# An RWKV layer rearranged: key products, paired tiles, triangular solves on another engine, merges on another DMA queue

## The chip, the cores and the metric

The kernel runs on one core of one Trainium2 chip. The metric is device time in microseconds of one launch. A core has TensorE (matrix products into PSUM), VectorE, ScalarE and GpSimd (elementwise work on SBUF; GpSimd doesn't read PSUM), SyncE, which here only issues DMAs, and 16 DMA engines. In the profile they are PE (its weight loads PEld), DVE, ACT, POOL and SP. Each engine works through its own list of instructions in order and waits on semaphores for the others.

## What is computed

The whole kernel is a decoder of two layers on 1024 positions of width 1024 in fp32: layer 0 with a gated linear recurrence, layer 1 with RWKV-7 time mixing, each followed by cross-attention into a memory and a squared-ReLU MLP. Only the time mixing matters here:

```
xx = x_prev - x
r = (x + xx * mu[0]) @ w_rkv[0];  k = (x + xx * mu[2]) @ w_rkv[1];  v = (x + xx * mu[3]) @ w_rkv[2]
w_log = -softplus(-(w0 + tanh(xw @ w1) @ w2)) - 0.5;  decay = exp(-exp(w_log));  a = sigmoid(a0 + (xa @ a1) @ a2)
kk = k * k_k, normalised per head;  k = k * (1 + (a - 1) * k_a)
rem_a, rem_b = -kk, kk * a
# per head and step:
sa = state @ a_t
state = state * w_t + sa b_t^T + v_t k_t^T
y_t = state @ r_t
```

The recurrence runs in chunks of 64 positions. For a chunk the mutual effect of the `a` and `b` vectors needs the inverse of a triangular 64x64 matrix per head. It is built from two 32x32 inverses, found by substitution (the "solves"), and an off-diagonal block, found by two small products (the "merges").

## The kernel before, in words

Everything lies transposed: 128 channels (two heads) by 1024 positions, so the 1024 channels are eight tiles f = 0..7. fp32 matrices are split into a rounded part and a rest, and each product is three matmuls (`mm3`, L304 to L306). `split` (L203 cast on ScalarE, L204 subtraction on VectorE) is used for weights and activations.

The layer's order is: low-rank maps; then for each tile f `decay(f)` (12 matmuls, the decay's running product `P`, its inverse `IP`, and `a`), `fphase` of k (48 matmuls: eight k-steps by three, for each half of the positions) and `prep(f, pk)`, which takes k from PSUM. `prep` makes `kk`, its square `sq` for the norm, `at` (minus kk times the decay before the position; L1181 and, for the first position of each chunk, L1182), `a` (a times kk times IP; L1179 and L1184 on GpSimd) and `kp` (L1175, L1176, and L1185 on GpSimd), and stores them for the scan. `sums(f)` puts eight matmuls against `ind` between those of the next tile (through the list `between`); `gram(f)` forms the 64x64 products (L1217), scales them by the norms (L1218, which waits for a small DMA into `db`) and stores the 32x32 blocks to `Ld` and `Mod`.

Then eight r tiles (the last two as a pair) and eight v tiles (the first two as a pair), each 48 matmuls; `evac_r` (L1325) multiplies by P and stores; `evac_v` transposes v (L1366), forms the bonus (L1358, then L1377, which needs r and k loaded back by `early`) and the gate. Then the scan, from L1555 on, over 16 chunks.

Before each of k, r and v the inputs are mixed: `rwkv_make_mix` makes the eight 512-wide pieces of one half of the positions in four groups (L1054 on ScalarE, L1055 and, in the second half, the one-column L1057 on VectorE, then `split`). A half's mix is called either through `later` (run between the two halves of a tile) or after a tile.

Aside from that run the solves, four of them (q = tiles 2q and 2q+1): `solve_load` (L1230, two memsets), `solve` (31 steps of two instructions, L1243 and L1245, and the copy L1246), `solve_store` (L1250, L1251); and the merges: `merge_load` (L1262 to L1264, per tile eight DMAs with 32x16 pieces of 128 bytes), `merge` (L1277, ScalarE copies, L1284), `merge_store` (L1292). `aside(step)` calls them at steps listed by hand: steps 0 to 7 follow the key tiles, 8 to 13 the first six r tiles, 14 the last pair, 15 and on the v tiles. Solve 0 runs on GpSimd, the others on VectorE. All their DMAs are issued by SP, whose queue also carries the weight tiles (L235), the loads of `early` and every store.

A scheduler orders each engine's list by a simulated timeline; `behind()` adds edges that put what it covers behind everything traced so far on the same engine. All 128x1024 tiles come from one pool of 45 buffers; weights are split two tiles ahead and loaded three ahead (`DA`).

Of the kernel before, what the change touches and what calls it, by code (L numbers as in the profile page):

```python
# [991 lines left out]


SL, SO, ST = (6, 7, 9, 11), (7, 8, 10, 12), (12, 10, 12, 14)
ML, ME, MS = (13, 11, 13, 15), (14, 12, 14, 16), (15, 13, 15, 17)
SE = [lambda nc: nc.gpsimd] + [lambda nc: nc.vector] * 3
# [6 lines left out]
def rwkv_consts(self):  # L1003
    nc = self.nc
    c = self.const
    self.omu = c([128, 48], "omu")
    nc.vector.tensor_scalar(self.omu, self.colv("mu", 48), -1.0, 1.0, ALU.mult, ALU.add)
    self.w0h = c([128, 8], "w0h")
    nc.vector.tensor_scalar(self.w0h, self.colv("w0"), 0.5, None, ALU.mult)
    self.a0h = c([128, 8], "a0h")  # L1010
    nc.vector.tensor_scalar(self.a0h, self.colv("a0"), 0.5, None, ALU.mult)
    self.kah = c([128, 8], "kah")
    nc.vector.tensor_scalar(self.kah, self.colv("k_a"), 0.5, None, ALU.mult)
    self.kam = c([128, 8], "kam")
    nc.vector.tensor_scalar(self.kam, self.colv("k_a"), -1.0, 1.0, ALU.mult, ALU.add)

    self.ind = c([128, 2], "ind")
    nc.gpsimd.memset(self.ind, 0.0)
    nc.gpsimd.memset(self.ind[0:64, 0:1], 1.0)
    nc.gpsimd.memset(self.ind[64:128, 1:2], 1.0)  # L1020

    self.id64 = c([128, 64], "id64")
    nc.vector.tensor_add(self.id64, self.ident[:, 0:64], self.ident[:, 64:128])

    self.mask1 = c([128, 128], "mask1")
    nc.gpsimd.memset(self.mask1, 1.0)
    self.mask2 = c([128, 64], "mask2")
    nc.gpsimd.memset(self.mask2, 1.0)
    for h in range(2):
        r = slice(h * 64, h * 64 + 64)  # L1030

        nc.gpsimd.affine_select(self.mask1[r, 0:64], self.mask1[r, 0:64], pattern=[[1, 64]], base=0,
                                channel_multiplier=-1, compare_op=ALU.is_ge, fill=0.0)
        nc.gpsimd.affine_select(self.mask2[r, :], self.mask2[r, :], pattern=[[1, 64]], base=-1,
                                channel_multiplier=-1, compare_op=ALU.is_ge, fill=0.0)
    self.db = c([128, 256], "db")
    self.pc = c([128, 128], "pc")

    self.ones = c([128, 128], "ones")
    nc.gpsimd.memset(self.ones, 0.0)  # L1040
    for h in range(2):
        nc.gpsimd.memset(self.ones[h * 64:h * 64 + 64, h * 64:h * 64 + 64], 1.0)


def rwkv_make_mix(self, X, i, hf):

    nc = self.nc
    out = []
    for j in range(KT // 2):
        m = self.unit()  # L1050
        for k in (2 * j, 2 * j + 1):
            o = (k % 2) * 512
            mu = self.col("mu", i * 8 + k)
            nc.scalar.activation(m[:, o:o + 512], X[hf][:, k, :], AF.Copy, scale=self.omu[:, i * 8 + k:i * 8 + k + 1])  # L1054
            nc.vector.scalar_tensor_tensor(m[:, o + 1:o + 512], X[hf][:, k, :511], mu, m[:, o + 1:o + 512], ALU.mult, ALU.add)  # L1055
            if hf:
                nc.vector.scalar_tensor_tensor(m[:, o:o + 1], X[0][:, k, 511:512], mu, m[:, o:o + 1], ALU.mult, ALU.add)  # L1057
        h, l = self.split(m)
        out += [(h[:, s], l[:, s]) for s in (slice(0, 512), slice(512, 1024))]
    return out  # L1060
# [31 lines left out]
def rwkv(self, X, xt, lw_wa, lw_g, post):  # L1092
# [20 lines left out]
    xk = []  # L1113
    for hf in range(2):
# [18 lines left out]
        xk.append(rwkv_make_mix(self, X, 2, hf))  # L1133
# [34 lines left out]
    def prep(f, pk):  # L1168
        cs = slice(f * 128, f * 128 + 128)
        c1 = lambda t: t[:, f:f + 1]  # L1170
        a, P, IP = dk.pop(f)
        kk = self.unit()
        nc.scalar.activation(kk, pk, AF.Copy, scale=self.col("k_k", f))
        kp = self.unit()
        nc.vector.tensor_scalar(kp, a, self.col("k_a", f), c1(self.kam), ALU.mult, ALU.add)  # L1175
        nc.vector.tensor_mul(kp, kp, pk)  # L1176
        sq = self.unit()
        nc.scalar.activation(sq, kk, AF.Square)
        nc.gpsimd.tensor_tensor(a, a, kk, ALU.mult)  # L1179
        at = kk  # L1180
        nc.vector.scalar_tensor_tensor(ch(at)[:, :, 1:], ch(kk)[:, :, 1:], -1.0, ch(P)[:, :, :63], ALU.mult, ALU.mult)  # L1181
        nc.vector.tensor_scalar(at[:, ::64], kk[:, ::64], -1.0, None, ALU.mult)  # L1182
        nc.sync.dma_start(MVd[:, f, 0, :], at)
        nc.gpsimd.tensor_tensor(a, a, IP, ALU.mult)  # L1184
        nc.gpsimd.tensor_tensor(kp, kp, IP, ALU.mult)  # L1185
# [3 lines left out]
        st_k[f] = sq, a, at  # L1189

# [36 lines left out]
    def solve_load(q):  # L1227
        sol[q] = [self.unit() for _ in range(3)]
        L, xt_, tmp = sol[q]
        nc.sync.dma_start(L, Ld[q].rearrange("b q h c s t -> (b q h c) (s t)"))  # L1230
        SE[q](nc).memset(xt_, 0.0)
        SE[q](nc).memset(xt_[:, ::33], 1.0)

    def solve(q):
# [5 lines left out]
        for s in range(31):  # L1240
            n, m = s + 1, 31 - s
            tv = tmp[:, :n * m].rearrange("p (j t) -> p j t", t=m)
            eng.tensor_tensor(tv, xv_[:, 0:n, s:s + 1].broadcast_to([128, n, m]),  # L1243
                              Lv[:, s:s + 1, s + 1:].broadcast_to([128, n, m]), ALU.mult)
            eng.tensor_tensor(xv_[:, 0:n, s + 1:], xv_[:, 0:n, s + 1:], tv, ALU.add)  # L1245
        eng.tensor_copy(tmp[0:64].rearrange("p (s j) -> p s j", j=32), xt_[0:64].rearrange("p (j s) -> p s j", s=32))  # L1246

    def solve_store(q):
        L, xt_, tmp = sol.pop(q)
        nc.sync.dma_start(Xd[q].rearrange("b q h c s t -> (b q h c) (s t)"), xt_)  # L1250
        nc.sync.dma_start(Xnd[2 * q:2 * q + 2].rearrange("q h c s t -> (q h c) (s t)"), tmp[0:64])  # L1251

    def merge_load(q):
        for f in (2 * q, 2 * q + 1):
            XT = self.unit()
            nc.vector.memset(XT, 0.0)
            XN = self.unit()
            xc = ch(XT)
            for h in range(2):
                for b in range(2):  # L1260
                    rs = slice(h * 64 + b * 32, h * 64 + b * 32 + 32)
                    nc.sync.dma_start(xc[rs, :, b * 32:b * 32 + 32], Xd[q, b, f % 2, h].rearrange("c s t -> s c t"))  # L1262
                nc.sync.dma_start(XN[h * 64:h * 64 + 32, 0:512].rearrange("p (c t) -> p c t", t=32), Xnd[f, h].rearrange("c s t -> s c t"))
                nc.sync.dma_start(XN[h * 64:h * 64 + 32, 512:1024].rearrange("p (c t) -> p c t", t=32), Mod[f, h])  # L1264
            mg[f] = XN, XT

    def merge(q):
        for f in (2 * q, 2 * q + 1):
            XN, XT = mg.pop(f)
            xc = ch(XT)  # L1270
            r0 = [slice(h * 64, h * 64 + 32) for h in range(2)]
            r1 = [slice(h * 64 + 32, h * 64 + 64) for h in range(2)]
            ps = self.bank()
            for c in range(16):
                s = slice(c * 32, c * 32 + 32)
                for h in range(2):
                    mm(ps[r1[h], s], XN[r0[h], 512 + c * 32:544 + c * 32], XN[r0[h], s], start=True, stop=True, tile_position=(h * 64, h * 64 + 32))  # L1277
            for h in range(2):
                nc.scalar.copy(XN[r1[h], 512:1024], ps[r1[h], :])
            ps = self.bank()  # L1280
            for c in range(16):
                s = slice(c * 32, c * 32 + 32)
                for h in range(2):
                    mm(ps[r0[h], s], XN[r1[h], 512 + c * 32:544 + c * 32], xc[r1[h], c, 32:64],  # L1284
                       start=True, stop=True, tile_position=(h * 64 + 32, h * 64))
            for h in range(2):
                nc.scalar.copy(xc[r0[h], :, 32:64], ps[r0[h], :].rearrange("p (c t) -> p c t", t=32))
            xts[f] = XT

    def merge_store(q):  # L1290
        for f in (2 * q, 2 * q + 1):
            nc.sync.dma_start(XTd[:, f, :], xts.pop(f))  # L1292

    def aside(step):

        for fn, steps in ((merge_store, MS), (merge, ME), (merge_load, ML), (solve_store, ST), (solve, SO), (solve_load, SL)):
            for q in range(4):
                if steps[q] == step:
                    with self.behind():
                        fn(q)  # L1300

    self.depth, self.ahead = DA
    xr, xv = [], []
    for f in range(8):
        decay(f)
        if f == 7:

            self.later.append(lambda: xr.append(rwkv_make_mix(self, X, 0, 0)))
        if f:
            sums(f - 1)  # L1310
        self.fphase(I["b_w_rkv"][0, 1], [f], xk, prep)
        if f:
            gram(f - 1)
        aside(f)


    xr.append(rwkv_make_mix(self, X, 0, 1))
# [10 lines left out]
    turns = [[f] for f in range(6)] + [[6, 7]]  # L1328
    for fs in turns:
        for f in fs:  # L1330
            early(f)
        if len(fs) > 1:
            self.later.append(lambda: xv.append(rwkv_make_mix(self, X, 3, 0)))
        if fs[0] == 0:
            sums(7)
        self.fphase(I["b_w_rkv"][0, 0], fs, xr, evac_r)
        if fs[0] == 0:
            gram(7)
        aside(8 + fs[0])


    xv.append(rwkv_make_mix(self, X, 3, 1))
# [181 lines left out]
    for fs in turns:  # L1524
# [3 lines left out]
        aside(14 + fs[-1])  # L1528
# [127 lines left out]
```

## Time and profile before

| | |
|---|---|
| median of 3 runs | 3068.84 us (3067.94 to 3074.63) |
| the profiled execution | 3074.59 us, its span 3072.8 us |
| mean granted TensorE clock | 0.970 |
| busy share | PE 94%, DVE 61%, ACT 44%, POOL 36% |
| RWKV key, r and v tiles up to the scan | 1424.6 to 1880.3 us of the span |
| key tile evacuated (L1173), tiles 0, 1, 2 | 1424.6, 1438.8, 1460.9 us |
| scan, its first W product to the last | from 1880.3 us, to about 2062 us |

In the rows, a line of the order of time has the start in us, the duration in us, engine, line, operation, out<-in (buffer numbers left out), shapes and count; in brackets, where there is one, the engine's idle time before it and what ended it. The granted clock is a share of TensorE's full speed: 1.00 is the level of 2.4 GHz, 0.50 that of 1.2 GHz.

### The profile page before, as it was taken

The numbers are of one execution on the slowest core, as the hardware profiler recorded it, in microseconds if no ns is written. First come the engines' busy times: TensorE is split into PE (matmuls) and PEld (weight loads), VectorE is DVE, ScalarE is ACT, GpSimd is POOL, SyncE is SP. The second block draws the span as 40 slices with busy tenths as digits, with TensorE's granted clock in tenths as the row PEclk, the third lists the DMA queues.
The fourth block names the chain that finished last, engine by engine and source line by source line (L and its number), as shares of the span: only waits on it lengthen the run. The fifth ranks groups of instructions, "written<-read, shape, count | busy, mean of one in ns | idle before, by whom it ended". The sixth has DMA issues, their size and how long they took to land.

```text
span 3072.8 us, 42865 instructions
## 1 busy us (share of the span) xinstructions
PE 2889.2 (94%) x16987; PEld 2394.9 (78%) x16987; DVE 1864.2 (61%) x2146; ACT 1344.2 (44%) x1915; POOL 1098.1 (36%) x909
## 2 busy tenths in 40 slices
PE   7999999898999999989987788989999899999998
PEld 6887898786888878867866666878788778887886
DVE  5576542637444778767788625884345644568776
ACT  5465342635454643355431523443334545454332
POOL 2000100015666744442461003662001466667442
PEclk9999999998999999999998899999999999999999
DMA  8213270123446644342664679872312245455443
GB/s 260 68 42 103 83 230 28 55 83 91 161 154 205 220 158 151 96 137 77 157 172 139 175 209 242 181 163 87 107 31 86 83 134 160 152 200 198 158 143 117
DMA packets 394921, 421.93 MB, mean 137 GB/s; under 512 B 103536, under 2 KB 305504, under 8 KB 394720
## 3 DMA queue, kind: packets, MB, share of 16 engines
q1 hardware_dynamic: 384720, 384.96, 42.4%
q0 software_dynamic: 9536, 33.64, 2.8%
q8 instruction: 134, 2.20, 0.3%
q14 instruction: 67, 0.55, 0.1%
q10 hardware_dynamic: 464, 0.59, 0.1%
HBM read 284.31 MB, written 134.74 MB: 136 GB/s over the span
## 4 chain that ended last, share of the span: by engine, by line
PE 54%; DVE 8%; issue 5%; POOL 4%; ACT 2%; DMA 2%; SPq 1%; POOLq 0%; DVEq 0%; ACTq 0%
PE q L304 12%; PE q L305 12%; PE q L306 12%; PE p L304 4%; PE p L305 4%; PE p L306 4%; DVE u L204 3%; PE q L1466 1%; ACT u L203 1%; DVE u L1245 1%; DVE u L1243 1%; DMA u<-d 1%; POOL u L1564 1%; PE q L1377 1%; DVE u L1577 1%
## 5 line engine op out<-in xcount | busy, mean ns | idle before, releaser
L204 DVE TENSOR_TENSOR u<-u,u 128x1024 fp32r<-128x1024 f32 (+1 forms) x518 | 812.2, 1596 | 351.4 <-ACT u L203 335.0
L304 PE MATMUL p<-u,u 128*128 128x512 f32 (+1 forms) x1920 | 722.2, 379 | 31.0 <-ACT u L203 26.3
L203 ACT CAST u<-u 128x1024 fp32r<-128x1024 f32 (+1 forms) x550 | 542.0, 1024 | 470.0 <-PE q L305 159.7
L305 PE MATMUL p<-u,u 128*128 128x512 f32 (+1 forms) x1920 | 721.0, 376 | 9.6 <-DVE u L204 9.6
L306 PE MATMUL p<-u,u 128*128 128x512 f32 (+1 forms) x1920 | 717.1, 374 | 3.8 <-DVE u L204 3.7
L304 PE MATMUL q<-u,u 128*128 128x512 f32 (+1 forms) x1632 | 643.9, 395 | 30.3 <-ACT u L203 9.2
L305 PE MATMUL q<-u,u 128*128 128x512 f32 (+1 forms) x1632 | 641.0, 393 | 6.4 <-DVE u L204 6.4
L306 PE MATMUL q<-u,u 128*128 128x512 f32 (+1 forms) x1632 | 635.8, 392 | 0.0
L304 PEld LDWEIGHTS p<-u,u 128*128 128x128 f32 x1920 | 368.7, 193 | 100.2 <-ACT u L203 31.8
L305 PEld LDWEIGHTS p<-u,u 128*128 128x128 f32 x1920 | 369.2, 192 | 76.1 <-DVE u L204 15.1
L306 PEld LDWEIGHTS p<-u,u 128*128 128x128 f32 x1920 | 369.1, 192 | 68.0 <-DVE u L204 5.8
L315 POOL TENSOR_SCALAR s<-s 128x1 f32<-128x1 f32 x98 | 37.2, 379 | 997.2 <-ACT u L313 996.2
L304 PEld LDWEIGHTS q<-u,u 128*128 128x128 f32 (+1 forms) x1632 | 309.4, 190 | 101.8 <-ACT u L203 13.9
L305 PEld LDWEIGHTS q<-u,u 128*128 128x128 f32 (+1 forms) x1632 | 309.9, 190 | 73.2 <-DVE u L204 8.7
L306 PEld LDWEIGHTS q<-u,u 128*128 128x128 f32 (+1 forms) x1632 | 309.7, 190 | 65.4 <-issue 0.4
L431 POOL TENSOR_TENSOR u<-u,u 128x1024 f32<-128x1024 f32 x64 | 179.2, 2822 | 84.8 <-DVE u L204 78.7
L975 DVE TENSOR_TENSOR z<-z,q 128x512 f32<-128x512 f32 x192 | 129.0, 681 | 94.2 <-PE q L306 93.8
L204 POOL TENSOR_TENSOR u<-u,u 128x1024 fp32r<-128x1024 f32 x32 | 95.1, 2971 | 166.3 <-ACT u L203 104.2
L411 POOL TENSOR_TENSOR u<-u,u 128x512 f32<-128x512 f32 x96 | 150.8, 1579 | 2.9
L304 PE MATMUL q<-z,u 128*128 128x512 f32 x256 | 102.6, 401 | 7.0 <-DVE u L610 7.0
L610 DVE SCALAR_TENSOR_TENSOR u<-p,s,u 128x1024 f32<-128x1024 f32 x24 | 30.8, 1284 | 122.3 <-ACT u L203 78.2
L204 DVE TENSOR_TENSOR u<-p,u 128x1024 fp32r<-128x1024 f32 x32 | 38.9, 1221 | 108.6 <-ACT u L203 108.6
(256 smaller groups left out, 3550.9 us busy)
## 6 DMA issues: line engine op xcount, KB each, us to landing
u<-d SPq DMA_DIRECT2D x201, 512.0 KB, 4.7
d<-u SPq DMA_DIRECT2D x113, 512.0 KB, 3.6
d<-u SPq DMA_DIRECT2D x132, 256.0 KB, 3.6
u<-in_m_w_up SPq DMA_DIRECT2D x64, 512.0 KB, 5.6
d<-u POOLq DMA_DIRECT2D x64, 512.0 KB, 4.3
u<-in_m_w_down SPq DMA_DIRECT2D x64, 512.0 KB, 6.0
u<-in_c_w_kv SPq DMA_DIRECT2D x32, 512.0 KB, 6.4
u<-d SPq DMA_DIRECT2D x56, 256.0 KB, 6.3
```

What stands on the lines that cost most here:

```text
L203: self.nc.scalar.copy(hv, src)
L204: (eng or self.nc.vector).tensor_tensor(lv, src, hv, ALU.subtract)
L304: mm(o, ah, bh, start=first, stop=False, **kw)
L305: mm(o, ah, bl, start=False, stop=False, **kw)
L306: mm(o, al, bh, start=False, stop=last, **kw)
L315: nc.gpsimd.tensor_scalar(v, ss, 1.0 / n, eps, ALU.mult, ALU.add)
L411: sub = lambda o, x, y: nc.gpsimd.tensor_tensor(o, x, y, ALU.subtract)
L431: self.nc.gpsimd.tensor_tensor(f[o][i], f[x][i], f[y][i], ALU.subtract)
L610: nc.vector.scalar_tensor_tensor(o, src, r, gb, ALU.mult, ALU.mult)
L975: nc.vector.tensor_add(to_, to_, o)
L1243: eng.tensor_tensor(tv, xv_[:, 0:n, s:s + 1].broadcast_to([128, n, m]), Lv[:, s:s + 1, s + 1:].broadcast_to([128, n, m]), ALU.mult)
L1245: eng.tensor_tensor(xv_[:, 0:n, s + 1:], xv_[:, 0:n, s + 1:], tv, ALU.add)
```

## The change

- Key products. `prep` is cut in two. `prep_head` makes `at` with a negated k_k column (`nkk`) and forms `IP * k` from PSUM at once; `prep_rest` makes `kp` (a scaled a times `IP * k`), `a` (one fused instruction), and multiplies `at` by the decay with one instruction, since minus is in already and the first position of a chunk needs nothing. GpSimd has no instruction left in it.
- Tiles. The last two key tiles and the first two r tiles run as pairs. `decay` runs one turn ahead. Half of the first r mix is built between the halves of the key pair, the rest, gram(5) and the second half's mix after `prep_head(7)` and ahead of `prep_rest(6)` and `(7)`; sums and grams of 6 and 7 move to the r tiles 2 and 3. Three of four groups of the first v mix are built in the last r pair, the fourth after it. The one-column piece of a mix moves from VectorE to ScalarE.
- Solves. Solves 0, 1 and 2 run on GpSimd, called behind key tiles 2, 4 and the key pair (their instructions are not put `behind`); their loads too are issued by GpSimd. Solve 3 stays on VectorE, its 31 steps spread one by one between the matmuls of r tiles 4 to 7; its memsets are on GpSimd.
- Merges. They go tile by tile, one per step: loads at steps 9 to 16, products one step later, stores one more. Steps 0 to 6 are now the key turns, 7 to 12 the r turns ([0, 1], 2, 3, 4, 5, [6, 7]), 13 to 19 the v turns. Memset, loads, stores of solves and merges are issued by GpSimd.

The diff, cut:

```diff
+TURNS = [[f] for f in range(6)] + [[6, 7]]
-SL, SO, ST = (6, 7, 9, 11), (7, 8, 10, 12), (12, 10, 12, 14)
-ML, ME, MS = (13, 11, 13, 15), (14, 12, 14, 16), (15, 13, 15, 17)
-SE = [lambda nc: nc.gpsimd] + [lambda nc: nc.vector] * 3
+SL, SO, ST = (2, 4, 6, 9), (2, 4, 6, 9), (2, 4, 6, 12)
+ML, ME, MS = range(9, 17), range(10, 18), range(11, 19)
+SE = [lambda nc: nc.gpsimd] * 3 + [lambda nc: nc.vector]
...
+            if hf:
+                nc.scalar.activation(m[:, o:o + 1], X[0][:, k, 511:512], AF.Identity, scale=mu, bias=m[:, o:o + 1])
             nc.vector.scalar_tensor_tensor(m[:, o + 1:o + 512], X[hf][:, k, :511], mu, m[:, o + 1:o + 512], ALU.mult, ALU.add)
-            if hf:
-                nc.vector.scalar_tensor_tensor(m[:, o:o + 1], X[0][:, k, 511:512], mu, m[:, o:o + 1], ALU.mult, ALU.add)
...
+    def prep_head(f, pk):
+        a, P, IP = dk[f]
+        at = self.unit()
+        nc.scalar.activation(at, pk, AF.Copy, scale=self.nkk[:, f:f + 1])
+        nc.vector.tensor_mul(IP, IP, pk)
+        dk[f] = a, P, IP, at
+
+    def prep_rest(f):
+        a, P, IP, at = dk.pop(f)
         kp = self.unit()
-        nc.vector.tensor_scalar(kp, a, self.col("k_a", f), c1(self.kam), ALU.mult, ALU.add)
-        nc.vector.tensor_mul(kp, kp, pk)
+        nc.vector.tensor_scalar(kp, a, self.col("k_a", f), self.kam[:, f:f + 1], ALU.mult, ALU.add)
         sq = self.unit()
-        nc.scalar.activation(sq, kk, AF.Square)
-        nc.gpsimd.tensor_tensor(a, a, kk, ALU.mult)
-        at = kk
-        nc.vector.scalar_tensor_tensor(ch(at)[:, :, 1:], ch(kk)[:, :, 1:], -1.0, ch(P)[:, :, :63], ALU.mult, ALU.mult)
-        nc.vector.tensor_scalar(at[:, ::64], kk[:, ::64], -1.0, None, ALU.mult)
+        nc.scalar.activation(sq, at, AF.Square)
+        nc.vector.scalar_tensor_tensor(a, a, self.col("k_k", f), IP, ALU.mult, ALU.mult)
+        nc.vector.tensor_mul(ch(at)[:, :, 1:], ch(at)[:, :, 1:], ch(P)[:, :, :63])
         nc.sync.dma_start(MVd[:, f, 0, :], at)
-        nc.gpsimd.tensor_tensor(a, a, IP, ALU.mult)
-        nc.gpsimd.tensor_tensor(kp, kp, IP, ALU.mult)
+        nc.vector.tensor_mul(kp, kp, IP)
...
+    def prep(f, pk):
+        prep_head(f, pk)
+        if f < 6:
+            prep_rest(f)
+        if f == 7:
+            rwkv_make_mix(self, X, 0, 0, xr[0], range(2, 4))
+            gram(5)
+            rwkv_make_mix(self, X, 0, 1, xr[1])
+            prep_rest(6)
+            prep_rest(7)
...
-        nc.sync.dma_start(L, Ld[q].rearrange("b q h c s t -> (b q h c) (s t)"))
-        SE[q](nc).memset(xt_, 0.0)
+        (nc.sync if q == 3 else nc.gpsimd).dma_start(L, Ld[q].rearrange("b q h c s t -> (b q h c) (s t)"))
+        nc.gpsimd.memset(xt_, 0.0)
...
+        for s in range(31):
+            if q == 3:
+                self.between.append(lambda s=s: one(s))
+            else:
+                one(s)
...
-                    nc.sync.dma_start(xc[rs, :, b * 32:b * 32 + 32], Xd[q, b, f % 2, h].rearrange("c s t -> s c t"))
+                nc.gpsimd.dma_start(xc[rs, :, b * 32:b * 32 + 32], Xd[f // 2, b, f % 2, h].rearrange("c s t -> s c t"))
...
-        for fn, steps in ((merge_store, MS), (merge, ME), (merge_load, ML), (solve_store, ST), (solve, SO), (solve_load, SL)):
+        for fn, steps in ((solve_load, SL), (solve, SO), (solve_store, ST), (merge, ME), (merge_load, ML), (merge_store, MS)):
...
-    for f in range(8):
-        decay(f)
+    decay(0)
+    for i, fs in enumerate(TURNS):
+        for f in TURNS[i + 1] if i < 6 else []:
+            decay(f)
+        if len(fs) > 1:
+            self.later.append(lambda: rwkv_make_mix(self, X, 0, 0, xr[0], range(2)))
+        if i:
+            sums(fs[0] - 1)
+        self.fphase(I["b_w_rkv"][0, 1], fs, xk, prep)
+        if 0 < i < 6:
+            gram(fs[0] - 1)
+        aside(i)
...
-    turns = [[f] for f in range(6)] + [[6, 7]]
+    for i, fs in enumerate([[0, 1], [2], [3], [4], [5], [6, 7]]):
...
+        if i in (1, 2):
+            sums(5 + i)
         self.fphase(I["b_w_rkv"][0, 0], fs, xr, evac_r)
+        if i in (1, 2):
+            gram(5 + i)
+        aside(len(TURNS) + i)
```

## Rows read from the trace of the kernel before

**Rows 1.** The page, part 1: busy time, share of the span, instructions.

```profile
PE 2889.2 (94%) x16987; PEld 2394.9 (78%) x16987; DVE 1864.2 (61%) x2146; ACT 1344.2 (44%) x1915; POOL 1098.1 (36%) x909
```

**Rows 2.** Stretches: length; busy PE, PEld, DVE, ACT, POOL; granted clock, DMA share, GB/s.

```profile
1424.60:1534.00 109.40, 104.26 (x753) 84.17 (x753) 81.49 (x68) 47.73 (x61) 48.76 (x18) 0.95 0.56 150
1534.00:1600.50 66.50, 57.65 (x389) 43.77 (x389) 51.27 (x64) 30.87 (x39) 41.23 (x37) 0.90 0.56 149
1600.50:1700.60 100.10, 75.22 (x601) 61.58 (x600) 84.72 (x201) 8.82 (x12) 24.58 (x34) 0.86 0.59 164
1700.60:1856.30 155.70, 135.55 (x1214) 103.76 (x1214) 67.13 (x89) 66.38 (x95) 5.12 (x4) 0.94 0.72 198
1856.30:1880.30 24.00, 11.86 (x59) 8.67 (x60) 9.34 (x18) 6.98 (x18) 9.65 (x11) 0.78 0.90 264
```

**Rows 3.** Waits of PE, 1424.6 to 1880.3: us in total, times, longest.

```profile
PE q L1377 <- DVE u L1358: 13.0, 2, 7.1
```

**Rows 4.** PE in order of time: ten matmul starts (first, last) and three waits.

```profile
1483.80 0.39 PE L305 MATMUL p<-u,u 128*128 128x512 f32 x1
...
1485.84 0.39 PE L305 MATMUL p<-u,u 128*128 128x512 f32 x1
...
1448.66 0.79 PE L304 MATMUL q<-u,u 64*128 64x512 f32 x1 [5.14 <-DVE u L1218]
...
1653.33 0.31 PE L1277 MATMUL q<-u 32*32 32x32 f32 x2 [10.59 <-DMA u<-d]
...
1707.34 1.22 PE L304 MATMUL p<-u,u 128*128 128x512 f32 x2 [13.74 <-ACT u L203]
```

**Rows 5.** SP's DMA issues in order of time: 32 merge loads (first, last), then weights.

```profile
1677.01 1.25 SPq L1262 DMA_DIRECT2D u<-d  x2
...
1694.54 0.48 SPq L1264 DMA_DIRECT2D u<-d  x1
...
1696.01 1.06 SPq L235 DMA_DIRECT2D u<-in_b_w_rkv  x2
```

**Rows 6.** DVE, then POOL, in order of time, in `prep(1)`.

```profile
1442.42 3.35 DVE L1181 SCALAR_TENSOR_TENSOR u<-u,u 128x1008 f32<-128x1008 f32 x1 [1.26 <-DMA d<-u]
1445.70 2.31 DVE L1182 TENSOR_SCALAR u<-u 128x16 f32<-128x16 f32 x1
...
1442.35 2.37 POOL L1185 TENSOR_TENSOR u<-u,u 128x1024 f32<-128x1024 f32 x1
1444.67 3.30 POOL L1184 TENSOR_TENSOR u<-u,u 128x1024 f32<-128x1024 f32 x1
```

**Rows 7.** DVE in order of time: two groups of a mix, split to split.

```profile
1556.75 1.23 DVE L204 TENSOR_TENSOR u<-u,u 128x1024 fp32r<-128x1024 f32 x1 [1.11 <-ACT u L203]
...
1560.41 1.23 DVE L204 TENSOR_TENSOR u<-u,u 128x1024 fp32r<-128x1024 f32 x1 [1.11 <-ACT u L203]
```

**Rows 8.** POOL in order of time, solve 0: first step, two between, last, copy.

```profile
1570.86 0.24 POOL L1243 TENSOR_TENSOR u<-u,u 128x31 f32<-128x31 f32 x1
...
1578.43 0.43 POOL L1245 TENSOR_TENSOR u<-u,u 128x112 f32<-128x112 f32 x1
...
1587.66 0.58 POOL L1245 TENSOR_TENSOR u<-u,u 128x207 f32<-128x207 f32 x1
...
1625.20 0.34 POOL L1245 TENSOR_TENSOR u<-u,u 128x31 f32<-128x31 f32 x1
1625.60 2.09 POOL L1246 COPY u<-u 64x1024 f32<-64x1024 f32 x1
```

**Rows 9.** ACT in order of time: key tile 2 taken from PSUM.

```profile
1460.89 1.11 ACT L1173 ACTIVATE u<-p,colt 128x1024 f32<-128x1024 f32 x1 [5.49 <-PE p L306]
```

**Rows 10.** DMA issues, columns: count, KB each, median us from issue to landing.

```profile
u<-d SPq DMA_DIRECT2D x201, 512.0 KB, 4.7
...
u<-d SPq DMA_DIRECT2D x64, 64.0 KB, 2.4
```

**Rows 11.** One line's instructions, GpSimd's DMA issue: ns min/median/max, first and last start.

```profile
L928 POOL DMA_DIRECT2D d<-u x32: 727/727/823, 769.0 to 2785.8; - x32
```

## What the change should do, and how that was worked out

> **What bounds the kernel now.** I read the busy shares first: TensorE is busy 94% of the span, VectorE 61%, GpSimd 36% [rows 1]. TensorE is the bound on average, so the change can win only where TensorE stands still or runs slowly. It touches the RWKV layer alone. I cut the part of that layer that it touches, from the end of the first key tile (1424.6 us) to the start of the recurrent scan (1880.3), into five stretches [rows 2]: key tiles 1 to 6; key tile 7 with r tiles 0 and 1; r tiles 2 to 7; the v tiles; what runs up to the scan.
>
> In each, length minus PE busy is idle time, and busy time times (1 - granted clock) is what the clock costs. The five rows give 10.4, 14.6, 35.4, 28.3 and 14.7 us, **103 us together** (71 idle, 32 clock). That is all that can be recovered here; outside, the instructions are nearly the same.
>
> What holds TensorE there, the waits and the order of time say. At 1448.66 it waits 5.1 us for L1218; at 1653.33 it waits 10.6 us for the loads of a merge; at 1707.34 it waits 13.7 us for a cast of weights [rows 4]. A further 13.0 us go to two releases of L1377, which are v tiles whose r and k were loaded late [rows 3]. Behind most of these stands the SP queue: merge loads take it from 1677.01 to 1695.02, 32 issues at 0.56 us, and only at 1696.01 is the next weight tile asked for [rows 5].
>
> **Part 1: key products.** Per tile three 128x1024 products leave GpSimd, an awkward pair (L1181, L1182) leaves VectorE, and two plain full-width products come to VectorE. What the old form costs stands in [rows 6]: L1181 starts at 1442.42, while GpSimd's L1185 runs to 1444.72, and ends 1.05 us after that. GpSimd's L1184, begun at 1444.67, needs 3.30 us instead of 2.37. L1182, 16 elements a partition, takes 2.31 us and ends when L1184 does. The two engines take turns, each waiting out the other's instruction. L1218 is queued behind this on VectorE and TensorE waits for L1218: the 5.1 us of rows 4 and the slow clock after it. In the changed kernel GpSimd is idle at that time, so of the 10.4 us of this stretch I take back 7 (0 to 10).
>
> VectorE's load there is 81.5 of 109.4 us [rows 2]. Per tile some 4.4 go (3.35 + 2.31 less 1.3 of work) and 2.5 come (two products at 1.23, the price of a two-input instruction of that width [rows 7]): 81.5 - 6 x 1.9 = 70. But from tile 3 on GpSimd solves, and each of eight wide or two-input instructions a tile may wait for one GpSimd step, 0 to 0.6 us [rows 8]: 0 to 19 more, so 70 to 89 of some 102. TensorE still covers that; the price is nothing while it does, and about what exceeds 102 if not.
>
> **Part 2: the joint of k and r.** With k tiles 6 and 7 paired, the second-half pass is 2 x 24 matmuls at 0.227 us (ten starts, first and last in [rows 4]), 10.9 us, under which half of the first r mix is built. One group of a mix takes 3.7 us (split to split [rows 7]), since cast and VectorE alternate. After the last key matmul six of eight groups remain, 22 us, beside 24 us of TensorE for r tiles 0 and 1 and gram(5). To this come the evacuation of the pair, 0 to 8 us of turns with GpSimd, and the last group's matmuls, 2.7. I put the remaining loss at 10 (4 to 16); now it is 14.6 in that stretch.
>
> **Part 3: solves on GpSimd.** This term decides. Solve 0 ran there from 1570.86 to 1625.54 [rows 8], 52.3 us without the 2.4 of the L1184 that runs between its steps, and contended all the while. Where VectorE stands back a step of 112 columns takes 0.43 us and one of 207 takes 0.58, a line of 0.25 + 0.0016 per column; over the 62 steps (10912 columns) and gaps of 0.08 that is 38 us. So the contended run was 1.38 times as long. The copy is 2.1.
>
> Key tile 2 is evacuated at 1460.89 [rows 9], about 1455 without the 5.1 us. Solve 0 then needs gram 1 and its scaling (an estimate of 10: 6.2 from L1181's start to TensorE's release in rows 4 and 6, and the products before), a store, a load that lands 4.7 after its issue [rows 10]: I start it at 1474. The solves follow one another in GpSimd's order: 3 x (38 + 2.1 + two stores at 0.73 [rows 11]) + two later loads at 5.4 = 136 us, so the third ends at 1610 without contention and at 1653 with 1.38 on all 114 us of steps. VectorE is dense under solves 0 and 1 and nearly empty under the third; I take 1638. Behind the third solve GpSimd's queue holds two memsets (1 us each, 0 to 2.1 by the copy's row; VectorE's solve 3 waits for the first) and the eight loads of merge 0. A DMA issue on GpSimd is 0.73 us for 256 pieces [rows 11]; in proportion to 512 short pieces it would be 1.45; I take 1.1 for each of eight, and 2.4 to land [rows 10]. So merge 0 can start **14 us later, at 1652** (1618 to 1671).
>
> When would TensorE be there? Key tiles 1 to 6 end at 1424.6 + 99 + 3; tile 7 and the last decay take 13.6, the joint's loss 10, gram(5) 2, r tiles 0 to 4 54.4, two sums and grams 6 (99 us for six tiles leave 2.9 a tile beside 60 matmuls): 1613. Merge 0 stands right behind r tile 4 in TensorE's order; in the kernel before, a merge stood there 10.6 us ahead of its data [rows 4]. So **39 us of a new wait** (5 to 58). r tiles 5 to 7 are queued behind it, and every v tile behind those; VectorE's wait for the memset falls in the same time.
>
> **Part 4: merges by tile on GpSimd's queue.** The waits of 10.6 and 13.7 us, with what the clock loses after them, go, and so does what holds the first late load of a v tile. Later merges are asked for a step ahead: 8 x 1.1 + 2 = 11 us of queue against 13 to 18 us a step. TensorE's and ScalarE's work for them is the same.
>
> The Trainium skill (DMA: Bandwidth & Descriptors, "Issuing engines are not separate DMA queues") says that transfers begun by different engines share the same DMA engines, and that spreading them saves only issue time, usually small. The trace disagrees with "usually small": 18 us on SP [rows 5]. By the page the 10.6 and 13.7 us would stay and the sum would be 1 us instead of the 25 below.
>
> **The sum.** New losses: 3 (key tiles), 10 (joint), 0 (other r tiles, without the new wait), 14 (v tiles: the second v mix is built after r as now, and DMA engines at 0.72 [rows 2] bring what is asked for earlier only partly earlier), 12 (up to the scan: the last r and k load still comes behind the scan's loads). That is 39 against 103, 64 us recovered; less the new wait of 39: **25 us faster** (6 to 59 by the wait alone, 0 to 65 with the bounds of joint and key tiles). The profiled execution took 3074.6 (span 3072.8 and 1.8 around it), so 3049.6. The median of the runs shown, 3068.8, lies 5.8 below that execution; with the same 25 it becomes **3044**.
>
> **Rivals.**
> - *GpSimd keeps up.* VectorE's dense stretches are short, the solves end near 1610 and TensorE waits 5 us: 59 us faster, 3010. For it: the steps of 0.43 and 0.58. Against it: VectorE at 74% in the key tiles.
> - *GpSimd starves: slower.* The solves alternate with a VectorE that is nearly always in a wide instruction, at a factor of 1.9 instead of 1.38: the third ends at 1610 + 0.9 x 114 = 1713, merge 0 begins at 1727, a wait of 114, 50 us slower, 3119. It decides when merge 0 comes after 1677, the third solve after 1663. The Trainium skill (GPSIMD Engine Reference, "Key points") states that GpSimd shares its SBUF interfaces with VectorE and contends with its two-input and two-port instructions; rows 6 agree.
> - *GpSimd's DMA issue is the slow queue.* At 2.0 us an issue a merge needs 18 us of queue against 13 to 18 a step: the first merge comes 7 us later, seven others 2.5 each. 25 us given back, no change, 3069. No row shows an issue of 512 pieces; for it speaks only the number of pieces, against it 0.73 us, nearly constant over 32 issues [rows 11].
>
> **How the numbers follow.** Forecast 0.58, keeps up 0.17, starves 0.17, slow issue 0.08. The predicted time is the first. Its own bounds are 3004 to 3069; the range takes in the other two that are no slower than now and leaves out most of the starving one: 3004 to 3074. A measurement of this kernel can tell about 0.2% (6 us) from no change. Faster: 0.55 of the 0.58 and 0.17, 0.72. Slower 0.18. Same 0.10.
>
> **What would show it.** Right: no wait for L1218 near 1448; no L1262 on SP; GpSimd's last L1243 between 1610 and 1655; one long idle of PE before the first L1277, released by a load, of 5 to 58 us; VectorE's turns longer in the key tiles with TensorE still full. Wrong: TensorE waiting for L1218 or splits in the key tiles (VectorE the bound there); a wait before every L1277 (the issue); casts that wait for a buffer that a late solve still holds; a last solve after 1663.

## The result, and the profile after

The changed kernel takes **3038.1 us** (3033.8 to 3040.9) against 3070.2 of the kernel before beside it: a ratio of 0.9892, 95% interval 0.9875 to 0.9910, so 28 to 38 us faster; 25 were forecast. Its profiled execution took 3040.9, 33.7 less than that of before. Of the ten executions of e10, further down, one took 6126.5 us and one 3077.3 at a granted clock of 0.914: its ratio contains the second, its median is hardly touched by either.

The page's part 1, which answers [rows 1]: VectorE is busy for 66 us less, GpSimd for 87 us more.

```profile
PE 2875.2 (95%) x16987; PEld 2383.3 (78%) x16987; DVE 1797.9 (59%) x1991; ACT 1349.3 (44%) x1939; POOL 1184.8 (39%) x1108
```

Five stretches again, with the columns of [rows 2] (length; busy PE, PEld, DVE, ACT, POOL; granted clock; DMA share; GB/s). They are bounded as there but for one: key tiles 6 and 7 are now emptied together, so the first ends where TensorE begins to stand for key tile 5.

```profile
1422.60:1524.90 102.30, 100.10 (x729) 80.25 (x726) 63.79 (x64) 42.72 (x58) 47.25 (x60) 0.97 0.54 150
1524.90:1605.40 80.50, 52.73 (x355) 41.17 (x356) 53.00 (x55) 30.95 (x44) 63.97 (x87) 0.84 0.41 115
1605.40:1683.60 78.20, 74.98 (x581) 60.10 (x581) 41.60 (x74) 18.94 (x24) 56.45 (x89) 0.97 0.75 222
1683.60:1823.30 139.70, 134.50 (x1278) 102.30 (x1278) 60.04 (x79) 61.17 (x93) 40.24 (x58) 1.00 0.83 232
1823.30:1847.30 24.00, 10.89 (x59) 8.20 (x59) 7.71 (x17) 7.00 (x17) 9.06 (x10) 0.84 0.81 226
```

The whole went from 455.7 to 424.7 us: 31.0 of the 33.7. Idle time and clock, counted as in the prediction, are now 5.2, 36.2, 5.5, 5.2 and 14.9 us, 67 in place of 103 (36 less; what is left of the lengths, PE's work at full speed, counts 5 us more). Forecast were 3, 10, 39, 14 and 12. So the sum was near, but **the loss is not where it was put**: the new wait of 39 was to stand in the r tiles, ahead of merge 0; it stands one stretch earlier, at key tile 5 and the joint. TensorE's waits over the five stretches (us in total, times, longest) say the same:

```profile
PE p L304 <- DVE u L1174: 21.3, 2, 13.0
PE q L1395 <- DVE u L1376: 7.2, 2, 7.0
...
PE q L1296 <- DMA u<-d: 3.2, 1, 3.2
```

L1174 is `prep_head`, the product that empties a key tile's PSUM; L1296 is the first matmul of a merge. The waits of 5.1, 10.6 and 13.7 us of [rows 4] and one of the two of [rows 3] are gone.

**The 13.0 us.** In order of time, GpSimd near the end of solve 0, then ScalarE, VectorE and TensorE at key tile 5:

```profile
1522.18 2.28 POOL L1260 TENSOR_TENSOR u<-u,u 128x112 f32<-128x112 f32 x1
...
1527.99 1.88 POOL L1270 COPY u<-u 64x1024 f32<-64x1024 f32 x1
1529.84 0.60 POOL L1271 DMA_DIRECT2D d<-u  x1
1530.43 0.56 POOL L1272 DMA_DIRECT2D d<-u  x1
...
1535.03 1.11 ACT L1173 ACTIVATE u<-p,nkk 128x1024 f32<-128x1024 f32 x1 [9.63 <-DMA d<-u]
...
1535.66 0.81 DVE L1180 TENSOR_SCALAR u<-u,colt,kam 128x1024 f32<-128x1024 f32 x1 [9.38 <-DMA d<-u]
...
1537.86 0.77 PE L304 MATMUL p<-u,u 128*128 128x512 f32 x1 [12.98 <-DVE u L1174]
```

ScalarE and VectorE stood 9.6 and 9.4 us, not for data but for a place to write: `at` and `kp` of tile 5 had been given two of solve 0's buffers (the trace names these two stores, L1271 and L1272, as what ended the two waits), and those are free when the stores land, some 5 us after 1529.84. Solve 0 took 52.5 us; with the prediction's 38 for an undisturbed one it would have ended near 1513 (an estimate). Its step of 112 columns shows the difference: 2.28 us here, 0.43 in [rows 8].

**The 8.3 us.** SP stood for the same tile's stores (L1186 is the last of them), so it asked late for the weights of an r tile; ScalarE waits for them, with the r mix queued behind it, and the emptying of the key pair behind that:

```profile
1542.88 0.63 SPq L1186 DMA_DIRECT2D d<-u  x1
1543.61 1.20 SPq L235 DMA_DIRECT2D u<-in_b_w_rkv  x1
...
1550.66 1.05 ACT L203 CAST u<-u 128x1024 fp32r<-128x1024 f32 x1 [11.57 <-DMA u<-in_b_w_rkv]
...
1556.49 1.22 DVE L204 TENSOR_TENSOR u<-u,u 128x1024 fp32r<-128x1024 f32 x1 [1.17 <-ACT u L203]
...
1560.99 1.22 DVE L204 TENSOR_TENSOR u<-u,u 128x1024 fp32r<-128x1024 f32 x1 [1.17 <-ACT u L203]
...
1563.40 0.79 PE L304 MATMUL p<-u,u 128*128 128x512 f32 x1 [8.33 <-DVE u L1174]
```

A group of the mix takes 4.5 us beside the second solve (split to split), against 3.7 in [rows 7].

**The solves and merge 0.** The three solves, each from its first step to its last (columns as in the stretches), then a step of 112 columns of the third, the first load of merge 0, and its first matmul:

```profile
1475.45:1527.93 52.48, 48.66 (x390) 39.00 (x390) 28.69 (x28) 17.05 (x23) 47.69 (x62) 1.00 0.40 106
1537.57:1591.83 54.26, 40.98 (x218) 31.15 (x218) 37.39 (x39) 26.46 (x39) 49.48 (x62) 0.89 0.31 74
1603.12:1643.88 40.76, 39.64 (x195) 32.53 (x196) 12.68 (x15) 4.20 (x4) 35.97 (x62) 0.96 0.85 260
```

```profile
1605.80 0.42 POOL L1260 TENSOR_TENSOR u<-u,u 128x112 f32<-128x112 f32 x1
...
1649.14 0.72 POOL L1283 DMA_DIRECT2D u<-d  x1
...
1654.72 0.21 PE L1296 MATMUL q<-u 32*32 32x32 f32 x2 [3.22 <-DMA u<-d]
```

They took 52.5, 54.3 and 40.8 us. VectorE was busy for 55%, 69% and 31% of that time, the DMA engines for 40%, 31% and 85%: the solves are long where VectorE is busy, not where the DMA engines are. The prediction had the start at 1474 (it is 1475), the third end at 1638 (1644, or 1646 with the copy), merge 0 at 1652 (1655). Only TensorE was not there 39 us ahead of it: the same GpSimd had already held it up by way of the buffers.

### The profile page after: what moved, and what is told of

Its sections match the earlier page's. It is cut to its first block, busy times and chain, and to the rows that moved or that the text cites. A ratio compares the mean times of both kernels' runs of the same rounds, so it can differ in the third digit from the quotient of the medians.

```text
span 3039.1 us, 42916 instructions
## 1 busy us (share of the span) xinstructions
PE 2875.2 (95%) x16987; PEld 2383.3 (78%) x16987; DVE 1797.9 (59%) x1991; ACT 1349.3 (44%) x1939; POOL 1184.8 (39%) x1108
## 5 line engine op out<-in xcount | busy, mean ns | idle before, releaser
L411 POOL TENSOR_TENSOR u<-u,u 128x512 f32<-128x512 f32 x96 | 150.9, 1581 | 2.9
L926 POOL TENSOR_TENSOR u<-u,u 128x512 f32<-128x512 f32 x32 | 46.1, 1441 | 163.9 <-ACT u L915 157.8
```

What stands on the lines that cost most here:

```text
L411: sub = lambda o, x, y: nc.gpsimd.tensor_tensor(o, x, y, ALU.subtract)
L926: tt(s1, r21, r22, ALU.add)
```

## The experiments

TensorE's way to the stretch differs between profiles with the same instructions ahead of it: key tile 0 is emptied at 1421.4 to 1429.9. So beside each run's time stands the length of **the stretch in its profile**, from the emptying of key tile 0 to the scan's first matmul: 455.7 us before, 424.7 after.

| run | time, us | ratio to before (95%) | stretch, us |
|---|---|---|---|
| changed kernel | 3038.1 | 0.9892 (0.9875 to 0.9910) | 424.7 |
| e1_short | 3027.2 | 0.9868 (0.9851 to 0.9884) | 406.0 |
| e2_keys | 3053.4 | 0.9951 (0.9937 to 0.9966) | 438.6 |
| e3_merge_sp | 3083.1 | 1.0047 (1.0032 to 1.0062) | 462.2 |
| e4_hold | 3038.6 | 0.9906 (0.9891 to 0.9921) | 425.8 |
| e5_hold2 | 3045.0 | 0.9919 (0.9901 to 0.9937) | 422.8 |
| e6_latecast | 3059.6 | 0.9966 (0.9953 to 0.9979) | 440.7 |
| e7_both | 3058.0 | 0.9959 (0.9943 to 0.9976) | 437.1 |
| e8_sp_vec | 3081.3 | 1.0040 (1.0028 to 1.0052) | 462.4 |
| e9_ahead | 3045.2 | 0.9912 (0.9891 to 0.9932) | 421.6 |
| e10_three | 3037.9 | 0.9904 (0.9876 to 0.9933) | 413.4 |
| e11_quiet | 3041.9 | one run | 421.2 |
| e12_less | 3040.1 | 0.9904 (0.9887 to 0.9921) | 425.2 |

### What the parts are worth: e2, e3, e8

**e2_keys**: the kernel before with `prep_head` and `prep_rest` of the diff in place of its `prep`, and `nkk`.

> The kernel before with the refactored key products alone (GpSimd's three products gone, two full-width ones on VectorE). By the prediction: 7 us faster than the kernel before, 0 to 10, so 3060 to 3070; the wait of 5.1 us for L1218 near 1448 gone. Rival: VectorE becomes the bound in the key tiles while the one solve runs on GpSimd beside it, and the gain is none or negative, 3070 to 3078.

15 us faster (10 to 19), twice what was priced. Key tiles 0 to 6 took 100.3 us, against 109.3 before: 9 us, within the bounds of 0 to 10. The rest is not in the key tiles. Key tile 0 and key tile 6 being emptied, the first step of solve 0, a step of solve 1 and its copy, and the first matmul of the first merge:

```profile
1422.51 1.12 ACT L1174 ACTIVATE u<-p,nkk 128x1024 f32<-128x1024 f32 x1 [1.51 <-PE p L306]
...
1522.85 1.11 ACT L1174 ACTIVATE u<-p,nkk 128x1024 f32<-128x1024 f32 x1 [3.41 <-PE p L306]
...
1539.96 0.24 POOL L1250 TENSOR_TENSOR u<-u,u 128x31 f32<-128x31 f32 x1 [30.61 <-DVE u L1057]
...
1601.07 0.38 DVE L1250 TENSOR_TENSOR u<-u,u 128x207 f32<-128x207 f32 x1
...
1630.15 1.12 DVE L1253 COPY u<-u 64x1024 f32<-64x1024 f32 x1
...
1636.28 0.24 PE L1284 MATMUL q<-u 32*32 32x32 f32 x2 [2.99 <-DMA u<-d]
```

In the kernel before, tile 7's products on GpSimd, the same step of solve 1 and its copy:

```profile
1566.21 2.38 POOL L1179 TENSOR_TENSOR u<-u,u 128x1024 f32<-128x1024 f32 x1 [21.91 <-ACT u L1178]
...
1612.45 0.69 DVE L1243 TENSOR_TENSOR u<-u,u 128x207 f32<-128x207 f32 x1
...
1647.22 1.01 DVE L1246 COPY u<-u 64x1024 f32<-64x1024 f32 x1
```

GpSimd's products of tile 7 no longer stand ahead of solve 0, which starts 31 us earlier than in [rows 8]. The first merge, though, is solve 1's, and solve 1 runs on VectorE; in the kernel before SP stood 14.2 us for its steps before it could store it and ask for the merge's loads. With solve 0 done sooner, VectorE's step of 207 columns takes 0.38 us in place of 0.69, solve 1 takes 42 us to its copy in place of 50 (from 1588.0 and 1597.2), and the wait of 10.6 us for the merge [rows 4] falls to 3.0. The prediction gave that wait to SP's queue, in part 4; most of it was the two solves taking turns. The rest of the change, on top of this part, is worth another 15 us (3053.4 to 3038.1).

**e3_merge_sp**: the changed kernel with the merges' transfers on SP's queue.

```diff
 def merge_load(f):
-                nc.gpsimd.dma_start(xc[rs, ...
+                nc.sync.dma_start(xc[rs, ...
...
 def merge_store(f):
-        nc.gpsimd.dma_start(XTd[:, f, :], xts.pop(f))
+        nc.sync.dma_start(XTd[:, f, :], xts.pop(f))
```

> The changed kernel with the loads and stores of the merges back on SP's queue, still tile by tile (the solves' own transfers stay on GpSimd's). By the prediction's part 4, SP's issues (8 of 0.56 us a merge, 4.5 us a tile) and SP standing behind the memset that GpSimd clears late push the weight loads back: 8 to 20 us slower than the changed kernel, 3046 to 3058. Rival: the gain of part 4 came from spreading the merges tile by tile and the queue hardly matters: within 4 us of the changed kernel, 3035 to 3042.

45 us slower than the changed kernel, and slower than the kernel before, where 8 to 20 were expected. The v tiles, from the last r tile's emptying to the last v tile's, take 167.1 us instead of 139.7; idle time and clock there are 28.0 + 8.3 us (the row; columns as in the stretches above) in place of 5.2. SP's issues around one v tile follow:

```profile
1689.43:1856.48 167.05, 139.04 (x1209) 104.60 (x1207) 66.77 (x95) 62.69 (x95) 10.58 (x10) 0.94 0.74 185
```

```profile
1773.29 2.85 SPq L1403 DMA_DIRECT2D d<-u  x4
1776.24 1.90 SPq L1282 DMA_DIRECT2D u<-d  x2
...
1781.38 0.42 SPq L1310 DMA_DIRECT2D d<-u  x1
...
1783.95 0.53 SPq L235 DMA_DIRECT2D u<-in_b_w_rkv  x1
```

The next weights (L235) come behind the merge loads (1776.2 to 1781.4), these behind the stores of the v tile before (L1403), which wait for its products. One such round takes 24 us, four times over; in the changed kernel such a v tile takes 17.6.

**e8_sp_vec**: the same, with the memset ahead of the loads on VectorE, since SP had stood 9.3 and 14.4 us behind a memset that GpSimd did late.

> The changed kernel with the merges' loads and stores on SP's queue as in the run of that name, and with the memset ahead of them on VectorE, as before the change. There SP stood twice (9.4 and 14.4 us) behind a memset that GpSimd did late. Theory Q1: that standing is most of the 45 us: 3045 to 3060. Theory Q2: the merges' transfers, in one order with stores that wait for the v tiles and ahead of the next weights, cost it by themselves: 3070 to 3086. If the queue mattered little without the memset: 3036 to 3043.

Within 2 us of e3: the memset is not the cause (Q2). What the engines do in what order changed with the queue too, ScalarE's casts coming behind the merge's copies; how much of the 43 to 45 us is SP's line and how much that order, these runs don't separate. The Trainium skill (DMA: Bandwidth & Descriptors, "Issuing engines are not separate DMA queues") says that starting DMAs from several engines saves only the time it takes to start them, usually small beside the transfers themselves. Both runs disagree with small: the merges cost 43 to 45 us on SP's queue, and their 72 issues of about 0.5 us make 36 (an estimate from the rows of e3).

### What GpSimd's slow solves cost: e1, e11

**e1_short**: the three solves on GpSimd cut short; the rest of each solve is left out.

```diff
-        for s in range(31):
+        for s in range(31 if q == 3 else 8):
```

> The changed kernel with GpSimd's three solves cut from 31 to 8 of their rows (16 of 62 instructions each; the rest of the solve is left out). Theory A: the two waits of TensorE for L1174 (13.0 and 8.3 us) come from solve 0, which takes 52 us beside a busy VectorE and whose buffers key tile 5 is given. Then a solve takes some 10 us, both waits go, the clock after them recovers, and the time is 3010 to 3020 us. Rival B: the waits belong to the joint of k and r itself (decay one tile ahead, the mix chain); then they stay and the time is 3032 to 3040.

11 us faster than the changed kernel by the medians, 7 by the ratios, 18.7 in the stretch (its scan begins 16 us earlier); the slowest of its four executions, 3031.3, lies below the changed kernel's fastest, 3033.8. The time is in neither of the two ranges. Of TensorE's two waits for L1174 one is gone; ScalarE's wait for weights ahead of the other follows:

```profile
PE p L304 <- DVE u L1174: 8.0, 1, 8.0
```

```profile
1539.69 1.05 ACT L203 CAST u<-u 128x1024 fp32r<-128x1024 f32 x1 [10.54 <-DMA u<-in_b_w_rkv]
```

So theory A holds for the wait of 13.0 at key tile 5, and B for the other: with short solves, too, ScalarE stands 10.5 us at the joint for weights that SP asks for behind the stores of tile 5.

**e11_quiet**: four of VectorE's products of `prep_rest` left out in key tiles 3, 4 and 5, so these tiles are not the reference's.

> The changed kernel with four of VectorE's products left out in key tiles 3, 4 and 5 (kp and the scalings of a and at; so the outputs of these tiles are not the reference's). By the prediction solve 0 is lengthened by taking turns with VectorE, 52.4 us against 40.4 of solve 2 beside a VectorE with little to do: with a third less VectorE work beside it, solve 0 takes 44 to 49 us. Rival: GpSimd's steps are that long of themselves, or by the DMA traffic: 51 to 54.

Solve 0, from its first step to its last (columns as in the stretches):

```profile
1480.72:1526.91 46.19, 46.19 (x362) 37.44 (x360) 17.82 (x19) 15.73 (x22) 41.40 (x62) 1.00 0.43 108
```

46.2 us with VectorE busy for 17.8, against 52.5 with 28.7, as taking turns has it. It is one run, and solve 0 varies from 48.8 (e3, e8, e9) to 55.1 (e5) in the other profiles with the full work, so the size of the effect is known only roughly. The cause shows more plainly within solve 0 of the changed kernel. Two steps of equal width, the second in a time in which VectorE stands for 14.7 us:

```profile
1499.13 1.54 POOL L1260 TENSOR_TENSOR u<-u,u 128x252 f32<-128x252 f32 x1
...
1507.80 0.65 POOL L1258 TENSOR_TENSOR u<-u,u 128x252 f32<-128x252 f32 x1
...
1521.17 0.69 DVE L1158 TENSOR_SCALAR u<-u 128x1024 f32<-128x1024 f32 x1 [14.72 <-ACT u L1157]
```

### Moving the buffers: e4, e5, e6, e7, e9, e10, e12

**e4_hold**: `ST = (3, 5, 7, 12)`, the stores one step later in the program.

> The changed kernel with the copy and the two stores of solves 0, 1 and 2 written one step later in the program; GpSimd's own order of work is the same, but the buffers of a solve are handed on one key tile later. Theory A': key tile 5 waited only because it was given the buffers of a solve still running; other buffers are free by then, the first wait (13.0) goes and most of the second: 3015 to 3026. Rival: with three buffers fewer in between, casts or the mixes get the late buffers instead: 3034 to 3045.

No change, as the rival had it. Key tile 5 still got the two buffers of solve 0 (the trace names the same two stores behind its waits); evidently no others were free. TensorE's two waits were 8.9 and 8.2 us.

**e5_hold2**: two steps later, `ST = (4, 6, 8, 12)`, with a one-element memset on L ahead of the copy.

> The changed kernel with the copy and stores of solves 0 to 2 written two steps later (one step later had changed no assignment of buffers: the same at and kp of key tile 5 got them), and with one-element memset on GpSimd ahead of the copy, so that all three buffers of a solve stay taken until then. GpSimd's order of work is as it was. Theory A: key tile 5 no longer waits for solve 0, nor does SP's load of weights: the first wait (13.0 us) goes, and the time is 3015 to 3027. Rival: with fewer buffers others become late, 3034 to 3043.

The expectation is wrong in one point: `aside` puts a step's stores behind its solve, so the copy of solve 0 came behind solve 1, at 1591.0, and its buffers were held for both. Key tile 5 no longer waited: it was emptied 95.8 us after key tile 0, against 112.5. But the time was no better. The loss came back at the joint and in the r tiles; VectorE and TensorE at the first place:

```profile
1591.10 2.36 DVE L1180 TENSOR_SCALAR u<-u,colt,kam 128x1024 f32<-128x1024 f32 x1 [7.20 <-POOL u L1270]
...
1595.83 1.44 PE L1230 MATMUL q<-u,u 64*64 64x64 f32 x22 [5.96 <-DVE u L1183]
```

L1270 is the memset ahead of solve 0's copy. `kp` of tile 7 waits for a buffer of that solve, and the gram for products queued behind it. The rival holds.

**e6_latecast**: at the joint, the split of r tile 1's weights behind the mix (`self.depth, self.ahead = (1, 2) if i == 6 else DA` ahead of the key tiles' `fphase`). **e7_both**: that with e5.

> The changed kernel with one thing altered at the joint: the cast and split of the weights of r tile 1 come one take later, behind the mix and not ahead of it. In the traces so far ScalarE stands 10.5 to 11.6 us at a cast L203 for weights that SP asked for late, with the mix of r queued behind it. Theory J: that is where the second wait (8.3 us) comes from; it goes or shrinks below 4, the first stays: 3026 to 3034. Rival: the mix chain itself sets the joint: 3035 to 3042.

> The edits of the two runs before it together. If the two waits have the two causes named there, the gains add up: 3008 to 3020. If both waits go back to the one lateness of solve 0, this is no faster than the later stores alone.

Both theories fall: 21 and 20 us slower than the changed kernel. In e6 the emptying of the pair is nearly in time (a wait of 2.0), but the cast, now behind the mix, comes late, and TensorE waits for it. The second store of solve 1, the cast, and TensorE:

```profile
1598.20 0.57 POOL L1272 DMA_DIRECT2D d<-u  x1
...
1602.45 1.99 ACT L203 CAST u<-u 128x1024 fp32r<-128x1024 f32 x2 [17.50 <-issue]
...
1603.55 0.80 PE L304 MATMUL p<-u,u 128*128 128x512 f32 x1 [12.10 <-ACT u L203]
```

The profile names nothing for ScalarE's 17.5 us. VectorE had finished the products of tiles 6 and 7 at 1594.5; the cast begins when that store, 4.2 us after its issue, lands. So it looks like one more buffer of a running solve, but that is not shown. e7 loses by several waits of up to 7.8 us, which were not followed.

**e9_ahead**: the load, not the split, is moved: `self.ahead = 2 if i == 5 else DA[1]`.

> The changed kernel with the weights of r tile 1 asked for one take earlier, ahead of key tile 5 (one buffer more is taken there). Theory K: the pair of key tiles takes two weight tiles at once, so the second load is asked for right ahead of its cast and ScalarE stands 11 to 13 us at that cast with the mix behind it; with the load earlier the second wait (8.3 us) goes and nothing else moves: 3026 to 3034. Rival: the one buffer more is missing elsewhere, or the mix chain itself sets the joint: 3035 to 3045.

The wait of 8.3 us at the joint is down to 1.1 and the one at key tile 5 to 4.3; 7 us slower all the same, 3 us shorter in the stretch: no gain that can be told. It came back at r tile 2, whose PSUM waited for an r tile's product, which stood on VectorE behind a split of weights that had been given a buffer of solve 1:

```profile
1604.54 1.23 DVE L204 TENSOR_TENSOR u<-u,u 128x1024 fp32r<-128x1024 f32 x1 [9.31 <-DMA d<-u]
...
1607.05 0.77 PE L304 MATMUL p<-u,u 128*128 128x512 f32 x1 [10.12 <-DVE u L1344]
```

**e10_three**: e5 and e9 and a 46th buffer, from constants that nothing reads.

> The changed kernel with the later stores of the solves, the earlier load of r tile 1's weights, and a 46th buffer won from constants that nothing reads (half of mask1, half of db, all of id64). If buffers are what moved the waits about in the runs before, the later stores now give back what they gave in the key tiles (9 to 16 us) without the losses after it, and the load another 5 to 8: 3012 to 3026. Rival: the losses move on, 3032 to 3045.

11 us shorter in the stretch, not in the time (3037.9). Seven of the 11 are a later start, key tile 0 being emptied at 1429.9 against 1422.6: the scan begins 4 us earlier. ScalarE and TensorE at its largest wait:

```profile
1587.09 2.00 ACT L1180 ACTIVATE u<-u 128x1024 f32<-128x1024 f32 x2 [16.75 <-POOL u L1268]
...
1588.19 2.08 PE L1206 MATMUL q<-ind,u 128*128 128x2 f32 x9 [17.07 <-ACT u L1180]
```

L1268 is that memset again, which this order puts behind solve 1: the square of a key tile waits for a buffer of solve 0 until 1587.

**e12_less**: four buffers fewer, with GpSimd's order kept: each `decay(f)` at its own turn, and the solves' scratch a constant of 256 columns.

> The changed kernel with four buffers fewer taken while GpSimd solves: a key tile's decay stands at its own turn, not one tile ahead (three), and a solve's scratch of 256 columns is a constant, its copy written over L (one). GpSimd's order is as it was. What was given solve 0's buffers in key tile 5 (at, kp) now gets others; they go to the decay of tile 7. If buffers that a running solve holds are what stops TensorE at key tile 5, the wait of 13.0 us goes and some of the joint's, with nothing taken from later tiles: 3022 to 3031. Rival: whatever is given those buffers next waits instead, as in the three runs before: 3034 to 3044.

Key tile 5 is emptied 81.3 us after key tile 0, with no wait, 31 us earlier than in the changed kernel (some of it because the decays of tiles 6 and 7 now come behind it). Yet r tile 1 is emptied 182.0 us after it, against 182.8: all of it was given back. ScalarE and TensorE at r tile 1, behind GpSimd's second store of solve 1:

```profile
1595.33 0.57 POOL L1273 DMA_DIRECT2D d<-u  x1
...
1599.74 1.04 ACT L203 CAST u<-u 128x1024 fp32r<-128x1024 f32 x1 [21.16 <-DMA d<-u]
...
1603.32 0.77 PE L304 MATMUL p<-u,u 128*128 128x512 f32 x1 [13.30 <-DVE u L1343]
```

A cast of weights had been given a buffer of solve 1 and stands 21 us for it (the trace names that store). So the theory of the buffers is right in its cause (what has a running solve's buffer waits for GpSimd) and wrong in its remedy: a buffer won at one place is missed at the next, as long as the solves end at about 1530, 1595 and 1645. e10, with a buffer more, did not shorten the measured time; only shorter solves (e1) did, and e1 leaves work out. No version with all the work beats the changed kernel by what can be measured.

## Why the prediction was right, and where it was not

- **The whole.** 25 us forecast, 32 measured, by a sum whose terms err in both directions: 26 us too few at the joint, 34 too many ahead of merge 0, 9 too many in the v tiles. That it came so near was in part luck. Its bounds of 0 to 65 take in the joint's alone; with those named for the key tiles they would be 7 us slower to 68 faster. 32 lies within both.
- **Part 1** was mis-sized. 7 us were taken back (0 to 10); alone it gives 15: 9 in the key tiles, the rest at the first merge. The step that failed: I counted the three products as contention in the key tiles and did not follow them in GpSimd's own order, where tile 7's stood ahead of solve 0 and so kept it running beside VectorE's solve 1, for which the merge waits. VectorE's load was about right: 70 us were forecast without a solve beside it (68.9 in e2), 70 to 89 with solves. The 63.8 of the first stretch hold the products of five key tiles, not six, at some 6 us each: the lower end. No wait for L1231 (the old L1218) over 1.4 us is left.
- **Part 2** was mis-sized. The joint was to lose 10 us (4 to 16). The second stretch loses 36.2, of which 13.0 are key tile 5's wait; about 23 remain, the slow clock after both waits included. Missing in the sum were the 11.6 us in which ScalarE stands for weights: a pair takes two weight tiles at once, so the second is asked for right ahead of its cast, and behind tile 5's stores. The group of the mix at 3.7 us was taken where no solve ran; beside one it is 4.5.
- **Part 3** was right in its times (start; length: 52.5 and 54.3 us contended, 52.4 by the factor of 1.38; 40.8 where VectorE stood back, 38 forecast) and in its main point, that GpSimd's late solves give back part of the gain. It was wrong about the way. It let TensorE run free to 1613 and then wait 39 us at merge 0. The wait there is 3.2; the first two stretches lose 41.4 us where 13 were forecast, 28 more. The failed step is that TensorE's arrival was counted from the tiles' work alone: the buffers that the solves hold, three at a time, were priced at nothing. The idle of 5 to 58 us before the first merge, listed as a sign of being right, is not there. The sign of the buffers stood in the list of what would show it wrong ("casts that wait for a buffer that a late solve still holds"), not in the sum. e1 gives the price: 11 us of time, 19 of the stretch, where the sum had 39.
- **DMA issue on GpSimd** was taken at 1.1 us; it is 0.51 to 0.72 for the loads of a merge. The rival of the slow issue falls, and so do the starving one and the one that keeps up: the third solve ended at 1644, neither after 1663 nor near 1610.
- **Part 4** was right about the v tiles and too small. They lose 5.2 us, not 14; put back on SP, the merges cost 43 to 45 us, by SP's line or by the order that changed with it. Of the two waits that it named, the 10.6 us were mostly not the queue's (e2). The 12 us up to the scan are 14.9: the last r and k load still comes late (the wait of 7.0).

## What to carry to other kernels

Where an engine off the critical path holds buffers of a pool that is full, its lateness reaches TensorE through whatever is given those buffers next; price a moved step by how long it holds buffers, not only by who reads its result. Moving such buffers about moved the wait; shortening the time they are held removed it at key tile 5. And before transfers go back onto a queue, look at what stands ahead of them and behind them in its order: a store that waits for an evacuation, with the next weights behind it, makes a round that no issue time shows.

## What the runs showed of the hardware

- A GpSimd step of 112 columns took 0.42 us beside a quiet VectorE and up to 2.28 beside a busy one, and a whole solve 40.8 against 52.5 and 54.3. It runs the other way too: VectorE's own step of 207 columns took 0.69 us beside GpSimd's solve 0 and 0.38 alone, and a mix group on VectorE and ScalarE went from 3.7 to 4.5 us.
- GpSimd's DMA issue takes 0.5 to 0.7 us for the merges' loads of many short pieces, no more than for the 256 pieces of [rows 11]. But some loads of a merge stood 3.7 to 6.5 us for nothing that the profile shows; no wait of TensorE's was traced to it.
